# Attention's value product with the values stationary in column halves, and the groups' weights formed beside the scores

## The chip, the cores and the metric

One Trainium2 chip, one of its cores. The time is device microseconds (us) of one launch of the whole kernel; the kernel before was run three times. The profile shows one further execution.

## The reference

One layer of a bidirectional encoder, 1024 tokens of width 1024, all float32. One input projection gives the attention's q, k and v, the inputs of a gated linear attention, and two merge gates. The change lies in the attention, 12 heads of 64 in three groups g of 4 heads, which look at keys that are 1, 4 or 16 tokens apart. Each group gives for every query and head a numerator (the sum of exp(score - max) times the value rows), a maximum m and a denominator den. The three groups are then combined:

```
for each group g:   s = q k^T / 8 + bias (masked);  m = max(s);  e = exp(s - m)
                    den = sum(e);   o = (e @ v) / den;   lse = m + log(den)
mix_w  = softmax(lse over the three groups)
y_attn = sum over groups of mix_w * o              # 1024 x 256
merged = sigmoid(gate_a) * (y_attn @ w_attn_branch) + sigmoid(gate_g) * (y_gla @ w_gla_branch)
x = LayerNorm(alpha * x + merged @ w_out);  x = LayerNorm(alpha * x + MLP(x))
```

The combination equals sum_g exp(m_g - m) num_g / sum_g exp(m_g - m) den_g, with m the largest of the three maxima: one factor per query, head and group.

## The kernel before

The big matrix products run as three matmuls each (lines 101 to 103: high and low parts of operands that were split in two), 128 rows by 512 columns at a time, into PSUM tiles `mm` in the projections and `ps` behind them. The last part of the projections is a list of steps; the attention is dealt out over these steps as `visit(i)`, so that its small matmuls stand between projection matmuls. A scheduler orders each engine's instructions from the dependencies, and the engines then work through their queues in order.

There are 24 attention tiles of 128 queries: eight of group 2, eight of group 1, eight of group 0, and `visit(i)` does a part of each of several tiles. `load` fetches q, k, v (POOL's DMA queue). `scores` does `sc` (line 803: keys stationary, 64 rows of the array for each head, two heads in the two row halves), the maximum on VectorE, exp on ScalarE. `turned` transposes the probabilities (`tr`, line 830) into `et`. `values` (line 844) multiplies: stationary are 128 columns of `et`, 64 value columns move, and `avp` gets [query, 4 heads x 64].

For groups 2 and 1 `values` copies `avp` and the statistics `sm` into a row `st` (lines 854, 855) and writes it to the DRAM buffer `rows` (lines 857, 859). For group 0 `turned` fetches the two other groups' rows into `R` (line 821), `weigh` (lines 881 to 884) and `blend` (lines 889 to 898) combine them on VectorE, `mixed` transposes the sum back on TensorE (line 872, two per tile), ScalarE copies it to `yat` (873) and POOL writes it to `yadr` (874).

After the last visits the projections go on for the steps that remain (VectorE adds, lines 631 and 642; SP writes `spill`, line 621). Then `branches` loads `ygdr` (the gated linear attention) and `yadr` (this attention) into six small tiles `pre` on SP's queue (line 963), splits them (lines 148, 149) into `yg` and `ya`, and the branch products `ps<-ya`, `ps<-yg` follow. The `pre` tiles take over memory of the attention's pool, tile by tile, and so wait for the last users of that memory.

Of the kernel before, what the change touches and what calls it, by code (L numbers as in the profile page):

```python
# [7 lines left out]
F32 = mybir.dt.float32  # L8
# [3 lines left out]
AF = mybir.ActivationFunctionType  # L12
OP = mybir.AluOpType
# [4 lines left out]
S = 1024  # L18
# [9 lines left out]
ORD = (1, 4, 8)  # L28
# [43 lines left out]
def build(tc, io):  # L72
    nc = tc.nc
    V, G, A, T, SP = nc.vector, nc.gpsimd, nc.scalar, nc.tensor, nc.sync
    P = Pools(tc)
    issued = {}
# [36 lines left out]
    rows = dr.tile([2, S, 264], F32, name="rows")  # L113
# [70 lines left out]
    for k in range(KT):  # L184
        n = {0: 1, 1: 1, 2: 2, 4: 2, 6: 2}.get(k)
# [18 lines left out]
    ident = cp.tile([128, 128], F32, name="ident")  # L204
# [12 lines left out]
    tp = trp.tile([128, 512], F32, tag="tr", name="tr")  # L217
# [491 lines left out]
    p0, p1 = projs[:2]  # L709
# [7 lines left out]
    a, b = p0["steps"][1], p0["steps"][4]  # L717
# [15 lines left out]
    ap_ = P.open("att", reuse_waits="tile")  # L733
# [17 lines left out]
    av = avp.tile([128, 256], F32, tag="av", name="avp")  # L751
    yat = ap_.tile([128, 2, 128], F32, name="yat")

    def window(g, t):

        if g == 2:
            return 128, 128, t * 128
        if g == 1:
            return (192, 256)[t % 2], (128, 0)[t % 2], t // 2 * 256
        return 192 if t in (0, 7) else 256, 128 if t == 0 else 64, min(max(128 * t - 64, 0), 832)  # L760

    def att(g, t):

        w, b0, k0 = window(g, t)
        b = {}
# [49 lines left out]
                                                 accum_out=sm[:, 4 + h:5 + h])  # L815

        def turned():
            if g == 0:
                b["R"] = R_t()
                for i in range(2):  # L820
                    G.dma_start(b["R"][:, 1 + i], rows[i, t * 128:t * 128 + 128])
            b["et"] = []
            nb = len(b["blks"])
            for i in range(2):
                tp, et = (x.rearrange("p a (b n) -> p a b n", n=128) for x in (tr_t(), et_t()))
                b["et"].append(et)
                for pr in range(2):
                    for j, (lo, hi, vv, p0) in enumerate(b["blks"]):
                        with tc.issue_after(issued["small"].ins):
                            T.transpose(tp[0:hi - lo, pr, j], b["e"][i][:, pr, lo:hi], ident)  # L830
                cpy = A.copy if i else V.tensor_copy
                if w == 192 and t < 7:
                    j = 0 if g == 0 else 1
                    cpy(et[0:64, :, j], tp[0:64, :, j])
                    cpy(et[:, :, 1 - j], tp[:, :, 1 - j])
                else:
                    cpy(et[:, :, 0:nb], tp[:, :, 0:nb])

        def values():
            nb = len(b["blks"])  # L840

            def part(j, h):
                lo, hi, vv, p0 = b["blks"][j]
                return T.matmul(av[:, h * 64:h * 64 + 64], b["et"][h % 2][p0:p0 + vv.shape[0], h // 2, j],  # L844
                                vv[:, h * 64:h * 64 + 64], start=j == h == 0, stop=j == nb - 1,
                                skip_group_check=True)

            with tc.issue_after(part(0, 0).ins):
                for j in range(nb):
                    for h in range(4):  # L850
                        if j or h:
                            issued["small"] = part(j, h)
            st = b["R"][:, 0] if g == 0 else st_t()
            V.tensor_copy(st[:, 0:256], av)
            V.tensor_copy(st[:, 256:264], b["sm"])
            if g == 1:
                G.dma_start(rows[0].rearrange("(u j c) w -> c u j w", u=2, c=4)[t // 2, t % 2], st)
            elif g == 2:
                G.dma_start(rows[1].rearrange("(j r) w -> r j w", r=8)[t], st)
            else:  # L860
                b["f"] = weigh(b["R"])

        def mix():
            if g == 0:
                b["o"] = o = st_t()[:, 0:256]
                blend(b["R"], b["f"], o)

        def mixed():
            if g == 0:
                tp = tr_t()  # L870
                for pr in range(2):
                    T.transpose(tp[:, pr, 0:128], b["o"][:, pr * 128:pr * 128 + 128], ident)
                A.copy(yat, tp[:, :, 0:128])
                G.dma_start(yadr[:, :, t * 128:t * 128 + 128].rearrange("b p n -> p b n"), yat)

        return load, scores, turned, values, mixed, mix

    def weigh(R):
        nm = R[:, :, 256:260]
        f = f_t()  # L880
        V.tensor_tensor(f[:, 3], nm[:, 0], nm[:, 1], op=OP.min)
        V.tensor_tensor(f[:, 3], f[:, 3], nm[:, 2], op=OP.min)
        V.tensor_tensor(f[:, 0:3], f[:, 3:4].to_broadcast([128, 3, 4]), nm, op=OP.subtract)
        A.activation(f[:, 0:3], f[:, 0:3], AF.Exp)
        return f

    def blend(R, f, o):
        den = R[:, :, 260:264]
        V.tensor_tensor(den, den, f[:, 0:3], op=OP.mult)
        V.tensor_tensor(f[:, 4], den[:, 0], den[:, 1], op=OP.add)  # L890
        V.tensor_tensor(f[:, 4], f[:, 4], den[:, 2], op=OP.add)
        V.reciprocal(f[:, 4], f[:, 4])
        V.tensor_tensor(f[:, 0:3], f[:, 0:3], f[:, 4:5].to_broadcast([128, 3, 4]), op=OP.mult)
        for g in range(3):
            num = R[:, g, 0:256].rearrange("p (h d) -> p h d", h=4)
            V.tensor_tensor(num, num, f[:, g].unsqueeze(2).to_broadcast([128, 4, 64]), op=OP.mult)
        V.tensor_tensor(R[:, 0, 0:256], R[:, 0, 0:256], R[:, 1, 0:256], op=OP.add)
        V.tensor_tensor(o, R[:, 0, 0:256], R[:, 2, 0:256], op=OP.add)
# [6 lines left out]
    gating = (turns([flat(e_t()) for _ in range(4)] + [flat(R_t()) for _ in range(2)], 6),  # L905
              turns([flat(et_t()) for _ in range(3)] + [gated[:, i] for i in range(3)], 6),
              turns([flat(kv_t()) for _ in range(3)], 3))

    def silu(h, hf):
# [15 lines left out]
        return load, do  # L925

    tiles = [att(g, t) for g in (2, 1, 0) for t in range(8)]

    issued["small"] = issued["pe"]

    def visit(i):

        for n, part in ((i + 1, 0), (i - 2, 3), (i, 1), (i - 1, 2), (i - 2, 5), (i - 3, 4)):
            if 0 <= n < 24:
                tiles[n][part]()


    n0 = len(steps) + 14
    for p in projs[2:]:
        steps += p["steps"]  # L940
    n1 = len(steps) - 7
    units = {}
    for i in range(27):
        units.setdefault(n0 + 1 + i * (n1 - n0) // 27, []).append(lambda i=i: visit(i))
    for i in range(8):

        n = n0 - 18 + i * 3 // 2
# [103 lines left out]
    w = []  # L1051
# [96 lines left out]
    w = [load_w(io["wo"][1, k2], [128, 2, 512]) for k2 in range(4)]  # L1148
# [241 lines left out]
    p0, p1 = pairs[:2]  # L1390
# [87 lines left out]
    R = {}  # L1478
# [326 lines left out]
```

## Time and profile before

| | us |
|---|---|
| median of 3 runs (lowest, highest) | 1380.91 (1380.14, 1382.19) |
| the profiled execution | 1383.76 |
| its span on the core | 1382.0 |
| TensorE busy (PE) | 1370.8 |
| VectorE busy (DVE) | 1011.3 |
| ScalarE busy (ACT) | 630.7 |
| GpSimd busy (POOL) | 99.1 |

The span is the time from the first to the last instruction; 1.8 us of the profiled execution lie around it. PE is TensorE's matmul stream, PEld its weight loads, which overlap matmuls. "SPq" and "POOLq" are the queues' own instructions, among them DMA issues. The end of a matmul is modelled, so the distance between the starts of two matmuls tells what one costs better than its duration does. The visits lie between 306 and 574 us of the span.

### The profile page before, as it was taken

To read this page: it belongs to the slowest core of one execution; us is meant where nothing else is said; L and a number is where in the kernel's file an instruction comes from. 1 tells how busy PE (TensorE), PEld (TensorE's weight loads), DVE (VectorE), ACT (ScalarE), POOL (GpSimd) and SP (SyncE) were. 2 spreads that over 40 slices of the span, in tenths; PEclk is the share of its full clock that TensorE was granted. 3 is DMA by queue.
4 is the path that set the end of the run, shared out by engine and by line. 5 is a ranking of instruction groups with operands and counts; after the bars stand their busy time and mean duration, and the time that the engine had idled before them with its cause. 6 is when DMAs were issued, how large, how long until landed. Compare 5 with 4: busy or idle time off the path is not lost.

```text
span 1382.0 us, 19028 instructions
## 1 busy us (share of the span) xinstructions
PE 1370.8 (99%) x6837; PEld 1153.0 (83%) x6837; DVE 1011.3 (73%) x1748; ACT 630.7 (46%) x1207; POOL 99.1 (7%) x153
## 2 busy tenths in 40 slices
PE   9999999999999999999999999999999999999998
PEld 6989998788888888888888888888888888888886
DVE  6377768677565677666667787878867897786988
ACT  5346645334344344354416655555556433333343
POOL 0000100013222232000001000000000000000002
PEclk9999999999999999999999999999999999999998
DMA  7262326575444443465753565666655965445313
GB/s 247 71 190 87 108 71 225 183 206 176 157 145 159 136 143 127 139 225 191 270 213 141 200 221 191 222 208 217 219 205 157 365 220 167 152 131 160 105 31 122
DMA packets 105907, 238.57 MB, mean 173 GB/s; under 512 B 20101, under 2 KB 28805, under 8 KB 105812
## 3 DMA queue, kind: packets, MB, share of 16 engines
q1 hardware_dynamic: 99220, 218.47, 47.4%
q0 software_dynamic: 6304, 18.49, 4.4%
q8 instruction: 54, 0.88, 0.3%
q10 hardware_dynamic: 288, 0.39, 0.1%
q14 instruction: 41, 0.34, 0.1%
HBM read 160.67 MB, written 77.68 MB: 172 GB/s over the span
## 4 chain that ended last, share of the span: by engine, by line
PE 90%; DVE 3%; DMA 2%; issue 2%; ACT 2%; POOL 0%; SPq 0%; POOLq 0%; ACTq 0%; DVEq 0%
PE ps L101 18%; PE ps L102 18%; PE ps L103 18%; PE mm L101 9%; PE mm L102 9%; PE mm L103 9%; PE avp L844 2%; PE tr L830 1%; PE sc L803 1%; ACT xr L1196 1%; DMA xrh<-in_xT 1%; DMA praw<-in_wfm 1%; PE sc L406 0%; PE tr L376 0%; DMA pwhi<-in_wfm 0%
## 5 line engine op out<-in xcount | busy, mean ns | idle before, releaser
L1177 ACT CAST T<-hp 128x1024 fp32r<-128x1024 f32 x36 | 37.8, 1051 | 107.6 <-PE ps L102 68.1
L102 PE MATMUL mm<-wlo,x 128*128 128x272 f32 (+1 forms) x240 | 74.5, 311 | 0.7 <-DVE wlo L94 0.7
L101 PE MATMUL mm<-whi,x 128*128 128x272 f32 (+1 forms) x240 | 75.0, 313 | 0.0
L103 PE MATMUL mm<-whi,x 128*128 128x272 f32 (+1 forms) x240 | 74.6, 311 | 0.0
L814 ACT ACTIVATE e<-e,sm 128x256 f32<-128x256 f32 (+2 forms) x96 | 43.4, 453 | 51.6 <-DVE sm L809 51.6
L102 PE MATMUL ps<-B,B 128*128 128x512 f32 x160 | 62.2, 389 | 0.0
L103 PE MATMUL ps<-B,B 128*128 128x512 f32 x160 | 62.2, 389 | 0.0
L101 PE MATMUL ps<-B,B 128*128 128x512 f32 x160 | 60.9, 390 | 0.5 <-ACT B L1177 0.5
L101 PE MATMUL ps<-T,T 128*128 128x512 f32 x144 | 56.0, 389 | 0.0
L102 PE MATMUL ps<-B,T 128*128 128x512 f32 x144 | 56.0, 389 | 0.0
L102 PE MATMUL ps<-T,T 128*128 128x512 f32 x144 | 56.0, 389 | 0.0
L103 PE MATMUL ps<-B,T 128*128 128x512 f32 x144 | 56.0, 389 | 0.0
L103 PE MATMUL ps<-T,T 128*128 128x512 f32 x144 | 56.0, 389 | 0.0
L101 PE MATMUL ps<-B,T 128*128 128x512 f32 x144 | 56.0, 389 | 0.0
L1578 DVE TENSOR_TENSOR acc<-ps,acc 128x512 f32<-128x512 f32 x68 | 45.8, 690 | 12.8 <-PE ps L103 12.2
L1178 DVE TENSOR_TENSOR T<-hp,T 128x1024 fp32r<-128x1024 f32 x36 | 44.1, 1224 | 14.1 <-ACT T L1177 14.0
L101 PE MATMUL mm<-x,pwlo 128*128 128x512 f32 x128 | 51.1, 399 | 1.4 <-DVE cu L642 1.4
L642 DVE TENSOR_TENSOR cr<-cu,mm 128x512 f32<-128x512 f32 x44 | 35.2, 800 | 23.3 <-PE mm L103 23.0
L1683 POOL TENSOR_TENSOR mv<-mv,mhalf 128x1 f32<-128x1 f32 x8 | 7.0, 880 | 607.3 <-DVE mv L1682 605.8
L103 PE MATMUL mm<-x,pwlo 128*128 128x512 f32 x128 | 50.0, 391 | 0.0
L102 PE MATMUL mm<-x,pwlo 128*128 128x512 f32 x128 | 50.0, 391 | 0.0
L101 PE MATMUL ps<-T,fraw 128*128 128x512 f32 x128 | 49.6, 390 | 0.4 <-ACT T L1177 0.4
(497 smaller groups left out, 4228.8 us busy)
## 6 DMA issues: line engine op xcount, KB each, us to landing
hdr<-c SPq DMA_DIRECT2D x112, 256.0 KB, 2.5
hp<-hdr SPq DMA_DIRECT2D x56, 512.0 KB, 3.6
spill<-cr SPq DMA_DIRECT2D x64, 256.0 KB, 3.0
praw<-in_wfm SPq DMA_DIRECT2D x16, 512.0 KB, 5.0
pwhi<-in_wfm SPq DMA_DIRECT2D x16, 512.0 KB, 4.6
gate<-spill SPq DMA_DIRECT2D x32, 256.0 KB, 3.7
wa<-in_w SPq DMA_DIRECT2D x16, 512.0 KB, 4.5
wb<-in_w SPq DMA_DIRECT2D x16, 512.0 KB, 6.4
```

What stands on the lines that cost most here:

```text
L101: T.matmul(ps, lh, rh, start=first and i == 0, stop=False, skip_group_check=more)
L102: T.matmul(ps, lh, rl, start=False, stop=False, skip_group_check=more)
L103: issued["pe"] = T.matmul(ps, ll, rh, start=False, stop=last and i == n - 1, skip_group_check=more)
L642: issued["add"] = V.tensor_tensor(o, a, b, op=OP.add)
L803: mm = T.matmul(sps[i][:, pr, 0:w], q[ps_, pr], k[ps_, pr, 0:w], start=True, stop=True)
L814: issued["exp"] = A.activation(e, e, AF.Exp, bias=sm[:, h:h + 1], scale=-1.0, accum_out=sm[:, 4 + h:5 + h])
L830: T.transpose(tp[0:hi - lo, pr, j], b["e"][i][:, pr, lo:hi], ident)
L844: return T.matmul(av[:, h * 64:h * 64 + 64], b["et"][h % 2][p0:p0 + vv.shape[0], h // 2, j], vv[:, h * 64:h * 64 + 64], start=j == h == 0, ...
L1177: A.copy(o[:, 0], src)
L1178: V.tensor_tensor(o[:, 1], src, o[:, 0].bitcast(F32), op=OP.subtract)
L1196: A.activation(q[i][:, k], tp[:, k], AF.Identity, bias=cols[:, c + 8:c + 9], scale=cols[:, c:c + 1])
L1578: V.tensor_tensor(m, p, m, op=OP.add)
```

## The change

In `values` the operands change places: 64 value columns are stationary, 128 columns of `et` move, and head h goes to column half h % 2 of the array, so that `av[64 i : 64 i + 64, pair]` holds the numerators with the head dimension on partitions. That is the layout in which `yadr` is kept, and the two transposes per tile of group 0 and their ScalarE copy go. Groups 2 and 1 write numerators to `numdr` and statistics to `smdr`, each by a DMA of its own.

For group 0 the factors of the three groups are formed from the statistics two steps behind the scores (`weigh`, `shares`); the other groups' statistics come by `stats` (two DMAs each at visits 12 and 16), their numerators by `quarter` (six DMAs at each of visits 17, 19, 21, 23) into one buffer `R`. Since the query is now on the free axis, the factors must be spread over partitions: `spread` transposes the 12 factors (one matmul, line 897), copies them (898) and writes them to `fdr`, and `loadw` reads them back over 64 partitions each into one buffer `W` (two DMAs). `values` then multiplies `av` out of PSUM into `W` (line 858), multiplies and adds the two other groups (865, 866), and writes `yadr` from `W` (867). There are 26 visits instead of 27.

```diff
-    st_t, R_t = ring(ap_, [128, 264], F32, 2, "st"), ring(ap_, [128, 3, 264], F32, 2, "R")
+    R, W = ap_.tile([128, 2, 2, 256], F32, name="R"), ap_.tile([128, 3, 2, 128], F32, name="W")
+    s12, fT = ap_.tile([128, 8, 2, 8], F32, name="s12"), ap_.tile([12, 128], F32, name="fT")
...
-                return T.matmul(av[:, h * 64:h * 64 + 64], b["et"][h % 2][p0:p0 + vv.shape[0], h // 2, j],
-                                vv[:, h * 64:h * 64 + 64], start=j == h == 0, stop=j == nb - 1,
+                return T.matmul(av[64 * i:64 * i + 64, pr], vv[:, h * 64:h * 64 + 64],
+                                b["et"][i][p0:p0 + vv.shape[0], pr, j], start=j == pr == 0, stop=j == nb - 1,
                                 skip_group_check=True)
...
-            st = b["R"][:, 0] if g == 0 else st_t()
-            V.tensor_copy(st[:, 0:256], av)
-            V.tensor_copy(st[:, 256:264], b["sm"])
+            if g:
+                st = st_t()
+                V.tensor_copy(st, av[:, 0:2])
+                G.dma_start(numdr[g - 1, :, :, t * 128:t * 128 + 128].rearrange("b p n -> p b n"), st)
+                return
+            V.tensor_tensor(W[:, 0], av[:, 0:2], W[:, 0], op=OP.mult)
+            for i in range(2):
+                c = ORD[i + 1]
+                n = 128 // c
+                num = R[:, i].rearrange("p b (c j) -> p b j c", c=c)[:, :, t % 2 * n:t % 2 * n + n]
+                wn = W[:, i + 1].rearrange("p b (j c) -> p b j c", c=c)
+                for pr in range(2):
+                    V.tensor_tensor(wn[:, pr], num[:, pr], wn[:, pr], op=OP.mult)
+                V.tensor_tensor(W[:, 0], W[:, 0], W[:, i + 1], op=OP.add)
+            G.dma_start(yadr[:, :, t * 128:t * 128 + 128].rearrange("b p n -> p b n"), W[:, 0])
...
-        def mixed():
+        def spread():
             if g == 0:
-                tp = tr_t()
-                for pr in range(2):
-                    T.transpose(tp[:, pr, 0:128], b["o"][:, pr * 128:pr * 128 + 128], ident)
-                A.copy(yat, tp[:, :, 0:128])
-                G.dma_start(yadr[:, :, t * 128:t * 128 + 128].rearrange("b p n -> p b n"), yat)
+                with tc.issue_after(issued["small"].ins):
+                    T.transpose(av[0:12, 2], b["f"][:, 0:3].rearrange("p g h -> p (g h)"), ident)
+                V.tensor_copy(fT, av[0:12, 2])
+                G.dma_start(fdr[:, t * 128:t * 128 + 128], fT)
+        def loadw():
+            if g == 0:
+                src = fdr.rearrange("(g b i) n -> i g b n", g=3, b=2)
+                for i in range(2):
+                    one = src[i, :, :, t * 128:t * 128 + 128]
+                    G.dma_start(W[64 * i:64 * i + 64], one.unsqueeze(0).to_broadcast([64, 3, 2, 128]))
+    def quarter(n):
+        u, q = n // 2, n % 2
+        for g in (1, 2):
+            c = ORD[g]
+            for pr in range(2):
+                src = numdr[g - 1, pr].rearrange("p (c u q j) -> p u q c j", c=c, u=2, q=2)[:, u, q]
+                dst = R[:, g - 1, pr].rearrange("p (c j) -> p c j", c=c)
+                for p in range(0, 128, 128 // g):
+                    ps_ = slice(p, p + 128 // g)
+                    G.dma_start(dst[ps_], src[ps_])
```

POOL's queue near the end of group 0, before. Lines 770 are loads of q and k, 791 and 792 of v, 821 of the other groups' rows, 874 writes the result.

```order
L795 DMA av1_2252<-vdr_86 128x2x256
L770 DMA ak1_2250<-spill_78 128x2x192
L821 DMA R1_2269<-rows_83 128x264 x2
L791 DMA av2_2253<-vdr_86 128x256
L874 DMA yadr_82<-yat_2275 128x2x128
L792 DMA av2_2253<-vdr_86 64x256
L821 DMA R0_2268<-rows_83 128x264 x2
```

The same place of the changed kernel (773 loads q and k, 794, 795 and 798 load v):

```order
L798 DMA av1_2254<-vdr_88 128x2x256
L773 DMA ak1_2252<-spill_78 128x2x192
L924 DMA R_2268<-numdr_83 128x4x64 x2
L924 DMA R_2268<-numdr_83 64x8x32 x4
L867 DMA yadr_82<-W_2269 128x2x128
L899 DMA fdr_85<-fT_2271 12x128
L794 DMA av2_2255<-vdr_88 128x256
L795 DMA av2_2255<-vdr_88 64x256
L906 DMA W_2269<-fdr_85 64x6x128 x2
```

In the place of two row loads per tile stand six loads for every second tile, and per tile a write of the factors and two loads of `W`, which stand in one queue behind the write of the tile before.

VectorE's queue at the last tile, before. Line 854 takes the last value product out of PSUM, 896 to 898 combine, 642 are the projections' adds, 149 splits.

```order
L642 TENSOR_TENSOR cu0_2103<-cu0_2103,mm_2124 128x512
L854 COPY R1_2269<-avp_2274 128x256
L896 TENSOR_TENSOR R1_2269<-R1_2269,f1_2265 128x256
L897 TENSOR_TENSOR R1_2269<-R1_2269 128x256
L898 TENSOR_TENSOR st1_2267<-R1_2269 128x256
L149 TENSOR_TENSOR pwlo_2118<-pwhi_2112,pwlo_2118 128x512
L642 TENSOR_TENSOR cr1_2106<-cu0_2103,mm_2122 128x512
```

The same of the changed kernel (644 the projections' adds, 151 splits, 94 splits of weights):

```order
L644 TENSOR_TENSOR cu1_2106<-cu1_2106,mm_2124 128x512
L858 TENSOR_TENSOR W_2269<-avp_2276,W_2269 128x256
L865 TENSOR_TENSOR W_2269<-R_2268,W_2269 128x128 x4
L866 TENSOR_TENSOR W_2269<-W_2269 128x256
L644 TENSOR_TENSOR cr1_2108<-cu1_2106,mm_2125 128x512
L866 TENSOR_TENSOR W_2269<-W_2269 128x256
L644 TENSOR_TENSOR cr1_2108<-cr1_2108,mm_2126 128x512
L94 TENSOR_TENSOR wlo_5291<-raw_5287,whi_5289 128x768
L644 TENSOR_TENSOR cr2_2109<-cu1_2106,mm_2125 128x512
L94 TENSOR_TENSOR wlo_5355<-raw_5351,whi_5353 128x768
L151 TENSOR_TENSOR yg0_5010<-pre_5028,yg0_5010 128x512
```

The weighting (858) now stands behind a wait for `W`, and ahead of the projections' last adds and of the first split of `yg`; before, the last tile was combined a good while earlier. The last product's 8 calls on TensorE are followed by 43 projection matmuls, and then by the branch products of `yg`; before, the last transposes (872) are followed by 117 projection matmuls, and then by the branch products of `ya`.

SP's queue at the same place of the changed kernel (623 writes the projections' results, 997 loads `pre`):

```order
L623 DMA spill_78<-cr1_2108 128x512
L997 DMA pre_5028<-ygdr_80 128x512
L997 DMA pre_5032<-ygdr_80 128x512
L997 DMA pre_5049<-ygdr_80 128x512
L997 DMA pre_5053<-ygdr_80 128x512
L997 DMA pre_5073<-yadr_82 128x512
L997 DMA pre_5077<-yadr_82 128x512
```

Ahead of the first load stands the write of `cr1`, which comes from the second of the two adds that follow the weighting in VectorE's queue.

More of the change, by code (lines that the diff above doesn't have):

```diff
@@ L112, in build @@
     yadr = dr.tile([2, 128, S], F32, name="yadr")
-    rows = dr.tile([2, S, 264], F32, name="rows")
+    numdr = dr.tile([2, 2, 128, S], F32, name="numdr")
+    smdr = dr.tile([2, S, 8], F32, name="smdr")
+    fdr = dr.tile([12, S], F32, name="fdr")
     tdr = dr.tile([12, 128, 512], F32, name="tdr")
@@ L747, in build @@
     sm_t, f_t = ring(ap_, [128, 8], F32, 3, "sm"), ring(ap_, [128, 5, 4], F32, 2, "f")
-    st_t, R_t = ring(ap_, [128, 264], F32, 2, "st"), ring(ap_, [128, 3, 264], F32, 2, "R")
+    R, W = ap_.tile([128, 2, 2, 256], F32, name="R"), ap_.tile([128, 3, 2, 128], F32, name="W")
+    s12, fT = ap_.tile([128, 8, 2, 8], F32, name="s12"), ap_.tile([12, 128], F32, name="fT")
+    st_t = turns([R[:, 1, i].rearrange("p (b n) -> p b n", b=2) for i in range(2)], 2)
     sc_t = turns([scp.tile([128, 2, 256], F32, tag="sc", name="sc") for _ in range(2)], 2)
     tr_t = turns([trp.tile([128, 2, 256], F32, tag="tr", name="tr") for _ in range(2)], 2)
-    av = avp.tile([128, 256], F32, tag="av", name="avp")
-    yat = ap_.tile([128, 2, 128], F32, name="yat")
+    av = avp.tile([128, 3, 128], F32, tag="av", name="avp")
     def window(g, t):
@@ L817, in turned @@
         def turned():
[L818 to L821, printed above, removed]
             b["et"] = []
@@ L856, in values, with weigh @@
+        def weigh():
+            sm = b["sm"]
             if g == 1:
[L857 removed]
+                G.dma_start(smdr[0].rearrange("(u j c) w -> c u j w", u=2, c=4)[t // 2, t % 2], sm)
             elif g == 2:
[L859 removed]
+                G.dma_start(smdr[1].rearrange("(j r) w -> r j w", r=8)[t], sm)
             else:
[L861 removed]
@@ L878, in weigh @@
[L878 to L898, printed above, removed]
+                o = s12[:, t]
@@ new lines, in att, with stats @@
+        return load, scores, turned, values, weigh, shares, spread, loadw
+    def stats(g):
+        for u in range(2):
+            G.dma_start(s12[:, 4 * u:4 * u + 4, g - 1],
+                        smdr[g - 1, 512 * u:512 * u + 512].rearrange("(t p) w -> p t w", p=128))
+    def quarter(n):
[8 more added lines that the diff above has]
+                    G.dma_start(dst[ps_], src[ps_])
@@ L904, in build @@
     gated = ap_.tile([128, 3, 512], F32, tag="strip1", name="gated")
-    gating = (turns([flat(e_t()) for _ in range(4)] + [flat(R_t()) for _ in range(2)], 6),
+    gating = (turns([flat(e_t()) for _ in range(4)] + [R[:, i].rearrange("p b n -> p (b n)") for i in range(2)], 6),
               turns([flat(et_t()) for _ in range(3)] + [gated[:, i] for i in range(3)], 6),
@@ L931, in visit @@
     def visit(i):
-        for n, part in ((i + 1, 0), (i - 2, 3), (i, 1), (i - 1, 2), (i - 2, 5), (i - 3, 4)):
+        for n, part in ((i + 1, 0), (i - 1, 5), (i - 2, 3), (i, 1), (i - 1, 2), (i - 1, 6)):
             if 0 <= n < 24:
                 tiles[n][part]()
+        if i in (12, 16):
+            stats(2 if i == 12 else 1)
+        if i in (17, 19, 21, 23):
+            quarter((i - 17) // 2)
     n0 = len(steps) + 14
@@ L942, in build @@
     units = {}
-    for i in range(27):
-        units.setdefault(n0 + 1 + i * (n1 - n0) // 27, []).append(lambda i=i: visit(i))
+    for i in range(26):
+        n = n0 + 1 + i * (n1 - n0) // 27
+        units.setdefault(n, []).append(lambda i=i: visit(i))
+        for k, part in ((i, 4), (i - 1, 7)):
+            if 0 <= k < 24:
+                units.setdefault(n + 2, []).append(lambda k=k, part=part: tiles[k][part]())
     for i in range(8):
```

19 lines of the change are left out of this document (15 added, 4 removed).

## Prediction

> **What bounds the kernel now.** I read the page first, then the waits of TensorE, then the groups of line 844, then the timeline where value products run, and last the place where the attention's results are handed to the branch products.
>
> ```profile
> span 1382.0 us, 19028 instructions
> PE 1370.8 (99%) x6837; PEld 1153.0 (83%) x6837; DVE 1011.3 (73%) x1748; ACT 630.7 (46%) x1207; POOL 99.1 (7%) x153
> PE 90%; DVE 3%; DMA 2%; issue 2%; ACT 2%; POOL 0%; SPq 0%; POOLq 0%; ACTq 0%; DVEq 0%
> PE mm L101 <- DVE cu L642: 1.4, 1, 1.4
> PE tr L830 <- ACT yat L873: 0.9, 1, 0.9
> ```
>
> TensorE is busy for 99% of the span and 90% of the chain that ended last is its own. No wait of its in the middle is longer than 1.4 us. So a change counts by what it takes from TensorE's stream, less every new wait of TensorE; time saved on the other engines counts for nothing while they keep up. The waits name one thing that the change removes: 0.9 us for `yat`, the copy behind the last transposes.
>
> ```profile
> L844 PE MATMUL avp<-av,et 128*128 128x64 f32 x272 | 33.9, 268 | 0.0
> L844 PE MATMUL avp<-av,et 64*128 64x64 f32 x48 | 6.8, 279 | 0.0
> ```
>
> The value products are 320 matmuls. Their durations are modelled ends, so I price them by starts, in blocks, from the timeline (columns: start, time, engine, line, tile, shapes, count):
>
> ```profile
> 331.93 0.39 PE L101 MATMUL mm<-xT,pwlo 128*128 128x512 f32 x1
> 332.16 1.00 PE L844 MATMUL avp<-av,et 128*128 128x64 f32 x8
> 333.08 0.71 PE L803 MATMUL sc<-ak,aq 64*128 64x128 f32 x8
> 333.73 0.65 PE L830 MATMUL tr<-ident,e 128*128 128x128 f32 x4
> ...
> 446.52 1.89 PE L844 MATMUL avp<-av,et 128*128 128x64 f32 x16
> 448.35 1.13 PE L803 MATMUL sc<-ak,aq 64*128 64x256 f32 x8
> 449.41 1.09 PE L830 MATMUL tr<-ident,e 128*128 128x128 f32 x8
> ```
>
> A block of 8 takes 333.08 - 332.16 = 0.92 us, one of 16 takes 448.35 - 446.52 = 1.83: 0.115 us for each matmul, though only 64 columns move. The weights, 128 columns of them, set that pace. The scores beside them show what two halves of the array do: 8 matmuls with 128 moving columns take 333.73 - 333.08 = 0.65 us, less than 8 value matmuls with 64, since they stand in two row halves. With 256 columns they take 449.41 - 448.35 = 1.06; the further 0.41 over four pairs is 0.10 us for each pair and 128 columns. If the halves ran one after another it would be 0.82.
>
> **The value products.** 320 before, 320 after, now with 64 weight columns and 128 moving ones, in column halves. No row of before shows two column halves at work at once. The nearest row is that of the scores: two halves, 128 moving columns. By it a block of 8 takes 0.65, one of 16 takes 0.65 + 4 x 0.10 = 1.05. To that comes the change of the array's tiling on the way in, which the first scores show, since they have projections on both sides:
>
> ```profile
> 305.62 0.39 PE L101 MATMUL mm<-x,pwlo 128*128 128x512 f32 x1
> 305.84 0.39 PE L102 MATMUL mm<-x,pwlo 128*128 128x512 f32 x1
> 306.16 0.72 PE L803 MATMUL sc<-ak,aq 64*128 64x128 f32 x8
> 306.81 0.50 PE L103 MATMUL mm<-x,pwlo 128*128 128x512 f32 x1
> 307.14 0.39 PE L101 MATMUL mm<-xT,pwlo 128*128 128x512 f32 x1
> ```
>
> Projections start 0.22 us apart, but 0.32 before the scores and 0.33 behind them: about 0.10 for each change of tiling. At 332.16 the value block follows its projection after 0.23, so it pays none now. After: 0.75 for 8 (saves 0.17), 1.15 for 16 (saves 0.68). Eight tiles have 8, ten have 16: 1.4 + 6.8 = 8.2. Six have 16, of which 8 have 64 rows each (the 48 of the group above); their 64-row parts change the tiling once more, so I take 0.6 each: 3.6. Sum 11.8.
>
> In the changed order five of the blocks are split by 12 projection matmuls. A split cost nothing before; now each pays two changes (0.2), and the first pair's weights and the way out once more (another 0.2, the part of the 0.65 that is above four pairs of 0.10, namely 0.25): 5 x 0.4 = 2.0. Left: -9.8 us. The bounds: with no overlap at all the term is +2.9 (worked out below), and with half the time of now and no cost at the edges it is 320 x 0.115 / 2 = -18.4. I stay with the scores' row because it is the same engine in the same shape of halves.
>
> The Trainium skill, TensorEngine Tiling (Array Packing), Performance Considerations, names just this exchange for products with at most 64 moving columns, and gives it a factor of two: by that sentence alone the term would be the -18.4. The trace's edges (0.32 against 0.22) are why I don't take it.
>
> **Transposes.** Removed are two for each tile of group 0; added is one for the factors.
>
> ```profile
> L872 PE MATMUL tr<-ident,st x16: 270/271/328, 504.8 to 574.0; 128*128 128x128 f32 x16
> ...
> 573.63 0.39 PE L103 MATMUL mm<-x,pwlo 128*128 128x512 f32 x1
> 573.86 0.38 PE L872 MATMUL tr<-ident,st 128*128 128x128 f32 x2
> 573.99 0.48 PE L101 MATMUL mm<-x,pwlo 128*128 128x512 f32 x1
> 574.31 0.40 PE L102 MATMUL mm<-x,pwlo 128*128 128x512 f32 x1
> ```
>
> From 573.63 to 574.31 stand 0.68 us for one projection start of 0.23, the pair, and the next: 0.22 for a pair, eight pairs 1.8. The new transpose moves 128 columns into 12 of the array's; it lies between 0.11 (half a pair) and 0.11 + 0.2 with two changes of tiling; I take 0.2, since its tile is narrow: eight are 1.6. Net -0.2, with ends -0.9 and +0.7. The wait for `yat` goes too: -0.9. TensorE's stream: -9.8 - 0.2 - 0.9 = -10.9.
>
> **Other engines, at nothing.** VectorE loses the copies of statistics and the waits of them for `rows`, and gets small operations for the factors. It is at 73% and not on the chain, so neither gain nor cost; if that cover were gone, the small ones are 0.17 us each. POOL issues 84 DMAs where it issued 32. By the rows below, 0.55 to 0.72 each, the 52 more are some 29 to 37 us over 270 us of an engine that is busy for 7%. Queued behind them are loads of q, k and v, which are asked for a visit ahead.
>
> ```profile
> L821 POOL DMA_DIRECT2D R<-rows x16: 537/553/567, 380.5 to 549.9; - x16
> 544.69 0.72 POOL L874 DMA_DIRECT2D yadr<-yat  x1 [3.34 <-ACT yat L873]
> ...
> 553.83 0.72 POOL L874 DMA_DIRECT2D yadr<-yat  x1 [3.41 <-ACT yat L873]
> ...
> 575.14 0.72 POOL L874 DMA_DIRECT2D yadr<-yat  x1 [5.26 <-ACT yat L873]
> rows<-st POOLq DMA_DIRECT2D x16, 132.0 KB, 3.0
> R<-rows POOLq DMA_DIRECT2D x16, 132.0 KB, 2.5
> yadr<-yat POOLq DMA_DIRECT2D x8, 128.0 KB, 3.1
> pre<-ygdr SPq DMA_DIRECT2D x8, 256.0 KB, 4.0
> ```
>
> **The new wait inside.** The weighting (858) waits for `W`, which comes by two transfers in a row: the factors out (0.55 and a landing of about 2.5) and back (two issues, about 3). `W` is single, and its next load waits until `yadr` has been written from it (3.1). VectorE's queue stands meanwhile, the projections' adds among it. In the changed order five tiles leave only one to two us between the factors' write and the load of `W`, so 858 will stand about 2 us there. TensorE has three PSUM tiles of 12 matmuls (2.7 us each) in hand, so most is hidden. I take 1 us in all, between 0 and 4: the upper end is two tiles that exceed the cover by 2.
>
> **The new wait at the end.** Before, the last `yadr` is issued at 575.14 and the projections run to 600.71:
>
> ```profile
> 572.04 1.83 SPq L963 DMA_DIRECT2D pre<-ygdr  x4
> ...
> 582.29 2.18 ACT L148 CAST yg<-pre 128x512 fp32r<-128x512 f32 x4
> ...
> 600.48 0.39 PE L103 MATMUL mm<-x,px 128*128 128x512 f32 x1
> 600.71 0.39 PE L101 MATMUL ps<-ya,whi 128*128 128x512 f32 x1
> ```
>
> That is 25 us of cover, and branch products follow projections without a gap. After, the last value product stands 43 matmuls from the end of the projections: 43 x 0.227 = 9.8 us. Counted from the last transpose of the factors (31 matmuls, 7.0 us ahead of the last product), the projections end at 7.0 + 0.9 + 9.8 = 17.7. The copy of the factors stands in VectorE's queue behind an add, at about 4.6; write 0.55 + 2.5; load 2 x 0.7 + 3.0: `W` is there at 12.1. Then VectorE: 858 and two 866 at 0.42, four 865 of half the size at some 0.25, two adds:
>
> ```profile
> L896 DVE TENSOR_TENSOR R<-R,f 128x256 f32<-128x256 f32 x24 | 9.4, 421 | 0.2
> L642 DVE TENSOR_TENSOR cr<-cu,mm 128x512 f32<-128x512 f32 x44 | 35.2, 800 | 23.3 <-PE mm L103 23.0
> ```
>
> 3 x 0.42 + 1.0 + 2 x 0.8 = 3.9: 16.0. SP's write of `cr1` waits for that, and the first load of `pre` stands behind it: 0.3, then 4.0 to landing, the cast 0.6 (four took 2.18): 20.9. TensorE, done at 17.7, stands 3.2 us until the first high part, and a further 1.3 us in all while the low part and the next three pieces come one by one through ScalarE and VectorE. I take 4.5; with landings of 2.5 in place of 3 and 4 it is 2, with the transfers of `W` at 4 each and a second stall for `ya` it is 8.
>
> **Sum.** -10.9 + 1.0 + 4.5 = -5.4 us against the profiled execution (1383.76 with 1.8 around its span), which lies 2.85 above the median of the three runs. On the median: 1380.9 - 5.4 = 1375.5.
>
> **Rivals.**
> - *The end stays hidden, or the edges are free.* The 4.5 goes because the last `W` comes 4 us sooner or the branch products find other work, or the edges of the blocks cost nothing (-18.4 in place of -9.8). For it: the scores' edges may be due to their 64-row loads. Time: 1380.9 - 10.9 - 0.5 = 1369.5, down to 1364.
> - *The waits eat the gain.* End 8, inside 3: -10.9 + 11 = 0, 1381. For it: one buffer `W` in a loop of weighting with an add (3.1), write (0.7 + 3.1) and load (1.4 + 3.0), 11.3 us, where two tiles' writes to `yadr` now stand 9.1 us apart (544.69 and 553.83). Against it: the tiles are not all that close, and the three PSUM tiles take up some.
> - *The column halves do not run at once.* Slower. Each matmul then takes the 0.10 of 128 moving columns: 320 x 0.0125 = 4 saved, 24 blocks pay two changes (4.8) and the splits 2.0: +2.9 in place of -9.8, and with the rest +7.3: 1388. It decides from the point at which a block of 16 takes over 1.45 us, about half of the overlap gone. Against it: the row halves overlap fully.
> - *A weight load waits for the other half's stream.* Half the weight columns (0.057) and the stream (0.10) would add up: 0.157 for each of 320, +13.6 with the edges near +20, and the time about 1402. Against it: before, 128 weight columns and 64 moving ones fit into 0.115 with one set of rows, so loads already run under streams there. The Trainium skill, TensorE: Matmul & The Clock Gate, Part 3, says that a weight load overlaps a running matmul only if their row groups differ; the value blocks of before, all in one row group, speak against that.
>
> **How the numbers follow.** The forecast, 3 to 9 us less, has 0.47; the hidden end or free edges 0.20; the eaten gain 0.18; halves in turn 0.12; loads in turn 0.03. About 0.2% (2.8 us) is what a measurement of this kernel can tell from no change. Faster: 0.67, same 0.18, slower 0.15. The range goes from 1366, most of the hidden end's cases, to 1385, which holds the eaten gain and leaves out the halves in turn. The forecast's own range is 1372 to 1378.
>
> **What would show it.** In the timeline after: a value block of 16 from its start to the next block's in 1.1 to 1.2 us, and pairs of starts a few ns apart; if a block takes 1.8, the overlap is wrong. Among TensorE's waits: a new one of about 3 us of `ps` on ScalarE's or VectorE's `yg` near 590 us; none there means the hidden end, 8 the eaten gain. VectorE's idle time ahead of 858 with a DMA of `W` as its end shows the inner wait, and any wait of `mm` on an add (644) what of it reaches TensorE. The prediction is wrong in kind if those two waits exceed 11 us, or if value blocks grow.

## The result: 4.7% slower

The changed kernel takes 1445.94 us (median of 4 runs, 1444.94 to 1447.78), the kernel before 1380.59 beside it: ratio 1.0473, 95% interval 1.0455 to 1.0491. The prediction was 1375.5, between 1366 and 1385: wrong in its sign.

The page of the changed kernel, three lines: the span, the engines' busy time, and the clock that TensorE was granted in 40 slices.

```profile
span 1445.0 us, 19118 instructions
PE 1375.4 (95%) x6829; PEld 1139.8 (79%) x6829; DVE 1010.2 (70%) x1756; ACT 628.3 (43%) x1199; POOL 137.6 (10%) x205
PEclk9999999999999888789999999999999999999999
```

TensorE, at 99% before, has gaps. Its clock is below full only in the slices that hold them, some 480 to 660 us into the span, where group 0's tiles lie. The waits (us in total, times, longest) name the gaps:

```profile
PE avp L897 <- DVE W L858: 52.6, 7, 10.7
PE mm L101 <- DVE cr L644: 7.6, 3, 3.6
DVE W L858 <- DMA W<-fdr: 67.5, 6, 14.8
DVE W L865 <- DMA W<-fdr: 23.6, 2, 17.2
POOL R L924 <- issue: 29.8, 13, 4.1
```

Read from the bottom: POOL loses time ahead of its loads of R; VectorE stands 91 us for the loads of W; TensorE stands 52.6 us at the transpose of the factors (897), which waits for the weighting (858), and 7.6 at projection products whose add is late. After a long stop TensorE runs at half its pace, as the timeline and the granted clock show (0.50 from 656 to 661 us, 1.00 from 645 to 650 and from 662 to 667):

```profile
651.74 0.39 PE L102 MATMUL mm<-xT,pwlo 128*128 128x512 f32 x1
651.97 0.39 PE L103 MATMUL mm<-xT,pwlo 128*128 128x512 f32 x1
655.95 0.79 PE L101 MATMUL mm<-xT,pwlo 128*128 128x512 f32 x1 [3.59 <-DVE cr L644]
656.54 0.63 PE L102 MATMUL mm<-xT,pwlo 128*128 128x512 f32 x1
656.97 0.63 PE L103 MATMUL mm<-xT,pwlo 128*128 128x512 f32 x1
...
661.97 0.39 PE L103 MATMUL mm<-x,px 128*128 128x512 f32 x1
662.19 0.39 PE L101 MATMUL mm<-x,px 128*128 128x512 f32 x1
```

Starts 0.23 us apart before the stop are 0.43 apart for 5.7 us after it. Between neighbouring projection matmuls there are 62 such intervals in the trace, 12.3 us more than at full pace; counted by the granted clock TensorE worked some 31 us at 0.50, which costs 15.6. The account of the span: +52.6 + 7.6 stops, +12.3 half pace, 72.5 in all; the span grew by 1445.0 - 1382.0 = 63.0, so TensorE's own stream is about 9.5 us shorter, or 12.8 with the 15.6; some 2 us of either are smaller waits that it no longer has elsewhere. That part of the change works:

```profile
336.99 0.39 PE L103 MATMUL mm<-x,pwlo 128*128 128x512 f32 x1
337.31 0.66 PE L844 MATMUL avp<-et,av 128*64 128x128 f32 x8
337.89 0.71 PE L806 MATMUL sc<-ak,aq 64*128 64x128 f32 x8
...
502.93 0.39 PE L103 MATMUL mm<-xT,pwlo 128*128 128x512 f32 x1
503.25 1.09 PE L844 MATMUL avp<-et,av 128*64 128x128 f32 x16
504.27 1.14 PE L806 MATMUL sc<-ak,aq 64*128 64x256 f32 x8
```

A value block of 8 takes 337.89 - 337.31 = 0.58 us (0.92 before), one of 16 takes 1.02 (1.83), and the way in is 0.32 instead of 0.23. All 320 value matmuls together take 23.2 us from start to start instead of 36.1; less 0.09 for each of 29 ways in that is 10.3 us saved.

How late the transfers are, by the DMA issues (KB each, us from issue to landing), and POOL's queue over one tile and a half:

```profile
W<-fdr POOLq DMA_DIRECT2D x16, 192.0 KB, 6.6
R<-numdr POOLq DMA_DIRECT2D x8, 128.0 KB, 2.9
R<-numdr POOLq DMA_DIRECT2D x16, 64.0 KB, 2.5
yadr<-W POOLq DMA_DIRECT2D x8, 128.0 KB, 2.3
fdr<-fT POOLq DMA_DIRECT2D x8, 6.0 KB, 1.8
```

```profile
547.40 0.73 POOL L867 DMA_DIRECT2D yadr<-W  x1 [8.73 <-DVE W L866]
549.29 0.54 POOL L899 DMA_DIRECT2D fdr<-fT  x1 [1.16 <-DVE fT L898]
553.13 1.34 POOL L906 DMA_DIRECT2D W<-fdr  x2 [3.29 <-DMA fdr<-fT]
560.09 0.72 POOL L798 DMA_DIRECT2D av<-vdr  x1 [5.62 <-issue]
560.80 0.71 POOL L773 DMA_DIRECT2D ak<-spill  x1
563.66 0.79 POOL L924 DMA_DIRECT2D R<-numdr  x1 [2.15 <-DVE sm L812]
566.76 0.76 POOL L924 DMA_DIRECT2D R<-numdr  x1 [2.31 <-DVE f L881]
569.89 0.71 POOL L924 DMA_DIRECT2D R<-numdr  x1 [2.37 <-DVE f L892]
572.62 0.69 POOL L924 DMA_DIRECT2D R<-numdr  x1 [2.02 <-issue]
575.44 0.69 POOL L924 DMA_DIRECT2D R<-numdr  x1 [2.12 <-DVE f L890]
578.79 0.69 POOL L924 DMA_DIRECT2D R<-numdr  x1 [2.66 <-issue]
579.47 0.72 POOL L867 DMA_DIRECT2D yadr<-W  x1
594.46 0.73 POOL L867 DMA_DIRECT2D yadr<-W  x1 [10.41 <-DVE W L866]
```

W lands after 6.6 us. Of the six loads of R each starts some 3 us after the one ahead, though its instruction takes 0.7: from 563.66 to 579.47 the quarter holds POOL 15.8 us, and the write of `yadr` stands behind. The writes of `yadr`, one per tile, are 32.1 us apart over that quarter (547.40 to 579.47) and 15.0 without one (to 594.46).

### The profile page after: what moved, and what is told of

Its sections match the earlier page's. It is cut to its first block, busy times and chain, and to the rows that moved or that the text cites. A ratio compares the mean times of both kernels' runs of the same rounds, so it can differ in the third digit from the quotient of the medians.

```text
span 1445.0 us, 19118 instructions
## 1 busy us (share of the span) xinstructions
PE 1375.4 (95%) x6829; PEld 1139.8 (79%) x6829; DVE 1010.2 (70%) x1756; ACT 628.3 (43%) x1199; POOL 137.6 (10%) x205
## 4 chain that ended last, share of the span: by engine, by line
PE 53%; ACT 1%; DVE 1%; DMA 1%; issue 0%; POOL 0%; DVEq 0%; ACTq 0%
PE ps L101 17%; PE ps L102 17%; PE ps L103 17%; ACT xr L1230 1%; DMA W<-fdr 0%; PE ps L1227 0%; PE mm L101 0%; PE mm L102 0%; PE mm L103 0%; DVE acc L1720 0%; ACT T L1211 0%; DVE acc L1724 0%; ACT B L1211 0%; DVE sts L1663 0%; DVE acc L1662 0%
## 5 line engine op out<-in xcount | busy, mean ns | idle before, releaser
L101 PE MATMUL mm<-xT,pwhi 128*128 128x512 f32 x120 | 49.4, 412 | 4.0 <-DVE cr L644 4.0
L897 PE MATMUL avp<-ident,f 128*12 128x128 f32 x8 | 2.8, 354 | 52.6 <-DVE W L858 52.6
L101 PE MATMUL mm<-x,pwlo 128*128 128x512 f32 x128 | 51.4, 402 | 0.1
L103 PE MATMUL mm<-x,pwlo 128*128 128x512 f32 x128 | 50.7, 396 | 0.0
```

Of the source, the lines that this page charges most:

```text
L101: T.matmul(ps, lh, rh, start=first and i == 0, stop=False, skip_group_check=more)
L103: issued["pe"] = T.matmul(ps, ll, rh, start=False, stop=last and i == n - 1, skip_group_check=more)
L897: T.transpose(av[0:12, 2], b["f"][:, 0:3].rearrange("p g h -> p (g h)"), ident)
```

## The experiments

Each group of kernels ran on one chip beside the kernel before (1380.6 to 1381.4 there). Where no interval is given, the time is of a single run.

**The shared tile.** The factors' transpose goes into another PSUM tile:

```diff
-                    T.transpose(av[0:12, 2], b["f"][:, 0:3].rearrange("p g h -> p (g h)"), ident)
-                V.tensor_copy(fT, av[0:12, 2])
+                    T.transpose(tp[0:12, 0, 0:128], b["f"][:, 0:3].rearrange("p g h -> p (g h)"), ident)   # tp = tr_t()
+                V.tensor_copy(fT, tp[0:12, 0, 0:128])
```

> The transpose of the factors goes into a tile of the ring for transposes (tr) instead of a third part of avp, the value product's tile; all else as in the changed kernel. Theory A (TensorE stops because that transpose stands in its queue behind the reader of the same avp tile, and that reader, the weighting on VectorE, waits for W): the seven stops of 52.6 us go, and with them most of the 62 matmuls at half pace (12 us): 1446 becomes 1382 to 1395. Theory B (VectorE's queue stands for W 91 us all the same, so the projections' adds come late and TensorE stops for its PSUM tiles mm instead): no more than 20 us less, 1425 to 1446, with long new waits of mm on the adds.

1444.5 us. Theory B: TensorE's waits only change their names.

```profile
PE avp L844 <- DVE W L858: 35.8, 6, 8.4
PE mm L101 <- DVE cr L644: 17.0, 5, 6.8
```

The next value product needs the same tile, and the adds stand behind the weighting in VectorE's queue. What TensorE waits at is a symptom; W is late.

**W from many places.** In `loadw` 63 of 64 partitions read `in_x` instead of one row set of the factors.

> W is loaded for one of 64 partitions from the factors (which keeps the wait for them), and for the 63 others from 63 different places of the input x, with the same runs of 512 B; the output is not the reference's, since 63 of 64 partitions get other weights. Theory C (the load lands late, 6.6 us, because 64 partitions read the same 3 KB of DRAM): the landing falls to about 3 us, VectorE's wait for W falls by some 8 x 3.6 = 29 us, and the time by 20 to 35 us to about 1415. Theory D (it lands late for its number of runs or its bytes): the landing stays at 6 to 7 us and the time within 8 us of 1446.

1453.25 us. The landing fell as theory C says, but not the time:

```profile
W<-in_x POOLq DMA_DIRECT2D x16, 189.0 KB, 3.8
```

```profile
629.28 0.88 POOL L908 DMA_DIRECT2D W<-in_x  x1 [2.18 <-DMA yadr<-W]
633.38 0.84 POOL L908 DMA_DIRECT2D W<-in_x  x1 [3.23 <-issue]
634.21 1.08 POOL L906 DMA_DIRECT2D W<-fdr  x2
```

POOL now put the second large load 4.1 us behind the first, so that the pair was there after 4.1 + 3.8 = 7.9 us, no sooner than the 0.7 + 6.6 of the changed kernel.

**R in plain loads.** `quarter` becomes one `G.dma_start(R[:, g - 1], numdr[g - 1].rearrange("b p n -> p b n")[:, :, n * 256:n * 256 + 256])` for each group.

> The six loads of R per quarter, 512 runs each, become two of 256 runs of 1 KB (the same bytes, in another order; the output is not the reference's, since numerators of other queries are weighted). Theory E (each of the six keeps POOL about 2.8 us, 17 us per quarter, so the writes of yadr, the factors and the loads of W behind them in POOL's queue come late): POOL's gaps ahead of R go, and the time falls by 10 to 25 us. Rival F (POOL's loss lies beside the wait for W's landing): under 5 us.

1419.16 us, 27 less: theory E, a little over its range's end.

**These three together.**

> The three edits together: factors' transpose in a tile of its own, W from different places, R in two plain loads; the output is not the reference's (weights of 63 of 64 partitions and numerators come from elsewhere). If late W by these causes and the shared tile are the whole loss, TensorE has no stop over 2 us left and the gain of its shorter stream shows: 1368 to 1376. If VectorE's standing for W is a cause by itself, 5 to 25 us more than that are left, with waits of mm on the adds.

1403.52 us, 22 over the kernel before: the second case, 2 us past its range. VectorE still waits 44 us for W (30.0 for the large loads, 14.0 for the small ones).

**The loop cut; R by another queue; the weighting later.** Four kernels. The first: the factors' transpose in `tr`, its copy on ScalarE, two W in turn (the second in memory that group 1 leaves free). The second: one word, `SP.dma_start` for `G.dma_start` in `quarter`. The third and fourth add to the first that ScalarE copies `av` to `o` in `values`, and a step `weight` a visit later works on it, with R on POOL and on SP.

> The factors' transpose goes into the ring tr and is copied by ScalarE, and W has two buffers in turn; the weighting stays where it is and R's loads stay on POOL. Theory L (a loop sets the pace: W lands, the weighting on VectorE, then the next tile's factors, whose copy and transpose stand behind it in both queues, their write, the next load of W, 15 to 17 us a tile where visits were 9 to 11 apart): the loop is cut, tiles without a load of R follow at the visits' pace, and the time falls by 20 to 45 us to 1400 to 1425. Rival M (it is the landing of W alone, 6.6 us, for which VectorE stands each time): under 10 us.

> The six loads of R per quarter go through SP's queue instead of POOL's, with the same runs; all else as in the changed kernel. Theory E (POOL's queue loses 2.8 us on each): as with two plain loads, some 27 us less, 1415 to 1425, and SP issues them in under 1 us each. Rival G (512 runs are slow to issue on any queue, or SP's writes of the projections' results then stand behind the wait for R): 1435 or more, with waits of mm on the adds or copies.

> As the cut loop, and ScalarE copies the group-0 product out of avp at once, while the weighting works on that copy a visit later (27 visits again); R's loads stay on POOL, each quarter after the visit that weights the tile before. Theory L with the landing: VectorE has a whole visit for W, its wait for W goes from 91 us to under 10, no stop of TensorE over 3 us is left, 1370 to 1385. Rival: POOL's 17 us per quarter still make W late for every second tile: 1390 to 1415.

> The same with R's loads on SP. If the losses were the loop and POOL's queue and nothing else, what is left is the shorter stream of TensorE, 10.9 us less than before by the prediction's sum: 1368 to 1374. If the value products' gain is smaller than the block times show, or SP's queue now holds the projections up, 1376 to 1395.

They took 1437.37, 1412.07, 1438.25 and 1408.93 us (the last a median of 4, ratio 1.0200, 1.0183 to 1.0217). So R's place in POOL's queue is worth 34 us, and SP issues four of the loads in 2.65 us:

```profile
458.36 2.65 SPq L924 DMA_DIRECT2D R<-numdr  x4
```

Cutting the loop is worth 9, less than theory L said and within rival M; weighting a visit later no more. The third and the fourth lie above both ranges that were given for each. In the last of them VectorE still waits for W:

```profile
PE mm L101 <- DVE cr L644: 20.6, 5, 6.8
DVE more L866 <- DMA more<-fdr: 28.0, 4, 11.3
DVE more L866 <- DMA W<-fdr: 16.1, 3, 6.6
```

A later step in the source is not a later place in the queue: the scheduler still set the weighting close behind the load of W (which `more`, the second W, shares), and W lands at 7.2 to 7.8 us.

**W taken away, on two queues, and in part.** In the last kernel W is loaded for the first two tiles only (`if t > 1: return`); then half of it through SP; and in the changed kernel with R on SP, W's rows of group 0 alone (`src[i, 0:1]`).

> As the version that weights a visit later with R's loads on SP, but W is loaded for the first two tiles of group 0 only (the six others are weighted with what stands there; the output is not the reference's); the factors' transposes, copies and writes stay. It leaves out the twelve later loads of W and every wait for them. If the waits for W are all that is left of the loss, no stop of TensorE over 1.5 us is left among the visits, none at half pace, and the shorter stream shows: 1368 to 1374, that is 7 to 13 us under the kernel before. If the column halves and the transposes do not give the 10.9 us of the prediction, or VectorE's and SP's added work cost something by themselves, 1376 to 1385.

> The version that weights a visit later with R's loads on SP, and half of each W (the other column half's partitions) goes through SP's queue too; the computation is whole. If the two loads of a W slow each other in POOL's queue (6.6 to 7.8 us with both under way), each lands in 3 to 5 us, VectorE's wait for W falls from 44 us to under 25, and the time from 1409 to 1385 to 1400. If SP's queue, which now waits for the factors, holds up the projections' writes, 1405 to 1425 with stops of TensorE on the adds or copies.

> As the changed kernel with R's loads on SP, but of W only the rows of group 0 are loaded for each tile, 64 runs x 2 rows, 64 KB in place of 192 per load; the output is not the reference's (the two other groups are weighted with stale factors). Theory D (W lands late for its bytes and runs): it lands in 2.5 to 4 us instead of 7.0, VectorE's wait for W falls by 25 us or more, and the time from 1412 to 1385 to 1400. Theory C (64 partitions that read one place are slow whatever the size): over 5 us, and over 1405.

Without the loads: 1380.52 us, ratio 0.9994 (0.9984 to 1.0003): the loss is gone, but not the 7 to 13 us under it. One long stop is left, at a transpose that waits for VectorE's copy of a tile, and ahead of that copy VectorE waited for R:

```profile
PE tr L906 <- DVE et L837: 5.6, 1, 5.6
```

```profile
DVE W L873 <- DMA R<-numdr: 2.7, 1, 2.7
```

Over two queues: 1413.30, and both halves landed late, in 8.0 and 8.7 us. A third of the bytes: 1391.53, landing in 3.4.

```profile
W<-fdr SPq DMA_DIRECT2D x4, 192.0 KB, 8.0
W<-fdr POOLq DMA_DIRECT2D x4, 192.0 KB, 8.7
```

```profile
W<-fdr POOLq DMA_DIRECT2D x16, 64.0 KB, 3.4
```

So it is not POOL's queue that makes W late: SP's half lands no sooner. Bytes, runs and the one place are left.

**Place and runs.** First, two queues and many places. Then the factors are kept so that each partition of W is one run of 3 KB; once in the changed kernel with R on SP, once in the kernel that weights later. (From the two-queue kernel on, the kernels that weight later also hold the weighting behind TensorE's last small product, `tc.issue_after(issued["small"].ins)`, which the kernel of 1408.93 us does not; no run shows what that alone is worth.)

```diff
-    fdr = dr.tile([12, S], F32, name="fdr")
+    fdr = dr.tile([8, 12, 128], F32, name="fdr")     # factors written in the order (half, group, pair)
...
-                    G.dma_start(W[64 * i:64 * i + 64], one.unsqueeze(0).to_broadcast([64, 3, 2, 128]))
+                    G.dma_start(W[64 * i:64 * i + 64].rearrange("p g b n -> p (g b n)"), one.unsqueeze(0).to_broadcast([64, 768]))
```

> The kernel with half of each W on SP's queue, and 63 of 64 partitions of each half read from different places of the input x (one from the factors, to keep the wait for them; the output is not the reference's). With all partitions reading one place each half took 8.0 to 8.7 us on either queue. Theory C (one place): the large loads land in 3 to 4.5 us on both queues with both under way, and the time falls from 1413 by 10 to 25 us. Theory D (bytes and runs): 6 us or more on both, 1405 or more.

> The changed kernel with R's loads on SP, and the factors kept in DRAM so that each partition of W is one run of 3 KB instead of six of 512 B; the computation is whole, the bytes and the place are the same. If the number of runs makes W late, it lands in 3 to 4 us instead of 7.0 and the time goes from 1412 to 1385 to 1400; if it is the bytes or the one place, 6 us or more and 1405 to 1415.

> The version that weights a visit later with R's loads on SP, with the long runs; the computation is whole. If runs are the cause, the waits for W nearly go, and the time comes to 1372 to 1385, near the 1380.5 of the version whose W stays; if not, it stays at 1405 to 1412.

Many places: 1380.42 us, the large loads through POOL landing in 4.3 (for those on SP the trace shows no landing); but here, as for three of the eight tiles in the first such run, the scheduler had put the large loads ahead of the factors' write, so the time says little. Long runs: 1383.76, 28 less than with short ones, all bytes and the one place as before:

```profile
W<-fdr POOLq DMA_DIRECT2D x16, 192.0 KB, 3.7
```

With the weighting later: 1376.05 (median of 10 runs, 1374.63 to 1380.59), ratio 0.9973, 0.9962 to 0.9984: faster than the kernel before by 0.27%, and the whole computation. Its longest wait among the visits:

```profile
PE mm L101 <- DVE cr L644: 2.3, 2, 1.3
```

**Halves in turn, and the long runs alone.** The first takes the alternation of halves from that kernel (`for h in (0, 2, 1, 3)`), the second puts only the long runs into the changed kernel.

> The version with long runs that weights a visit later, and the value products' heads in the order 0, 2, 1, 3, so that two neighbouring products go to one column half before two go to the other; the computation is whole. If the gain is the overlap of neighbours in different halves, half of the pairs no longer overlap: a block of 8 goes from 0.58 to 0.8 us or more, one of 16 from 1.02 to 1.5 or more, and the time rises by 3 to 9 us over 1376. If the blocks are shorter only because 64 weight columns load faster than 128, the block times and the time stay within 1.5 us.

> The changed kernel with the long runs for W and nothing else; R's loads stay on POOL. If the two causes are separate, W's landing is worth here what it was with R on SP, 28 us: about 1418. If R's 17 us in POOL's queue hide or set the lateness of W anyhow, 1430 or more.

1378.35 (median of 9; 0.9980, 0.9970 to 0.9990), not to be told from 1376.05, whose interval it overlaps; the 2.3 us lie between the two theories. The blocks stayed as they were, which the first theory excludes:

```profile
316.34 0.66 PE L845 MATMUL avp<-et,av 128*64 128x128 f32 x8
316.93 0.72 PE L807 MATMUL sc<-ak,aq 64*128 64x128 f32 x8
...
397.37 1.15 PE L845 MATMUL avp<-et,av 128*64 128x128 f32 x16
398.44 1.14 PE L807 MATMUL sc<-ak,aq 64*128 64x256 f32 x8
```

0.59 and 1.07 us. That does not speak against the overlap. Line 1738 of the changed kernel multiplies in plain float32, as the value products do, on the whole array, and its matmuls of 512 moving columns start 0.43 us apart: 0.107 for 128 columns, so eight one after another would need 0.86. And the starts in the blocks come in pairs, 0.007 us apart in the changed kernel (503.247 and 503.254, then 503.407) and mostly 0.011 to 0.014 here, with about 0.11 from pair to pair. So two halves do run at once here too; the order in the source is not what lets them. The long runs alone: 1416.93, 29 less, as forecast. The two causes add up:

| R's loads | W in short runs | W in long runs |
|---|---|---|
| POOL | 1445.9 | 1416.9 |
| SP | 1412.1 | 1383.8 |

Long runs are worth 29.0 and 28.3, R on SP 33.9 and 33.2, and the later weighting on ScalarE's copy, with two W and the hold behind the small product, another 8 (1376.05).

## Why the prediction was wrong, step by step

- *The value products* (11.8 less 2.0): right. Blocks of 0.58 and 1.02 with 0.09 for the way in stand beside the 0.75 and 1.15 that were worked out from the scores' rows, and all blocks together save 10.3 where the sum had 9.8. With the transposes the stream was to be 10.9 shorter, and the account of the span leaves 9.5 to 12.8. The rivals with halves or loads in turn are out by these blocks.
- *Loads under streams*, the argument against the last rival, was misread. In the blocks of before nearly every weight load starts 0.055 us behind a matmul and the next matmul 0.055 behind the load (446.800, 446.856, 446.912), and 64 columns take 0.054 by the rate of line 1738: load and stream may as well take turns there, so the 128 weight columns need not set the pace of 0.115 alone. In the blocks after, a load starts with the matmul ahead of it (337.469 behind 337.467) and the pairs still follow at 0.11, what 128 moving columns take alone. So loads do run under matmuls with all rows in use there, against the rule that the prediction quoted from the Trainium skill, TensorE: Matmul & The Clock Gate, Part 3.
- *Other engines, at nothing*: failed at POOL. The 24 loads of R were priced at their issue, 0.55 to 0.72; each kept the queue some 3 us. That is 33 us of the 65 (R on SP).
- *The new wait inside* (1, between 0 and 4): the step that failed. By the prediction's own sign, two waits over 11 us, it was wrong in kind: they are 52.6 and 7.6. First, the load of W was priced at 3 us to landing, from rows of transfers in 128 to 256 runs of 0.5 to 1 KB, none from one place; it took 6.6 (long runs: 28 us of the 65). Second, the cover was taken to be the projections' three PSUM tiles, but the factors' transpose and the next value product stand in TensorE's own queue behind the weighting of the tile before, so TensorE stopped at those. Third, a tile's lateness is handed to the next in a loop, which the prediction had as a rival with 11.3 us a turn; it turned in 15 to 17 without R and 30 to 36 with it. This third part is the small one: cutting the loop was worth 9, and with R on SP the cut and the later weighting together 3 to 8, so what each turn paid was mostly W's own landing.
- *The end* (4.5, 2 to 8): a stop of 3.6 and some 2.6 at half pace behind it (13 intervals of 0.2 more). It lies at a projection product, whose add stands behind 858, and no branch product waited, which the prediction would have read as the hidden end. The place was wrong, and that the size came out within the range is luck: the half pace in it was no term.
- *Half pace after a stop*, 12.3 to 15.6 us, was no term at all.
- *The rival "the waits eat the gain"* named the place and the loop, but its price was 11 us, where the stops and what follows them are 72.5 or more.
- *The rival "the end stays hidden"* takes off 0.5 that no row gives: with the prediction's own terms it is 1380.9 - 10.9 + 1.0 = 1371.0, not 1369.5.

## What to carry to other kernels

Price a new transfer by its shape (how many runs, of which length, from how many places) and not by the nearest transfer of like bytes, and put its whole chain in a row: from the value to its landing, against the time between turns. If an engine's queue stands for a landing at every turn, any excess is paid at every turn. Where many partitions read the same few KB, lay them out so that each partition reads one long run; here that was worth 28 us.

## What the runs showed of the hardware

- W in 384 runs of 512 B from one place of 3 KB landed in 6.5 to 9.1 us, on either queue (medians of the runs); in 128 such runs in 3.4; in 64 runs of 3 KB from the same place in 3.4 to 3.8; in 378 runs of 512 B from many places in 3.8 to 4.4. Many short runs and one place together are slow; why, these runs don't show.
- On POOL a load of 512 runs made the next of its kind wait until about 3 us after its start, on SP it didn't (some 0.7 us each).
- In the changed kernel's trace TensorE's granted clock fell to 0.50 seven times between 480 and 662 us, for 6.8 or 10.2 us each, two or three times 3.41. Each time it fell during a stop of 3.98 us or more between starts; stops of 2.06 and 3.51 left it at 1.00. In the two-queue run a stop of 2.36 us was followed by 3.4 us at 0.50, so the length of one stop alone does not decide. In the changed kernel matmuls ran at half pace for 3.1 to 5.9 us after these stops. The Trainium skill, TensorE: Matmul & The Clock Gate, Part 1, gives an idle window of about 3.4 us for this, and as long a busy one for the way back; the stretches, whole multiples of 3.41 us, agree with such a window, and the way back took up to 5.9.
